# A two-layer decoder trunk on one core: c is copied whole from its PSUM bank, and the planner's price of a product gets 32 columns more

## The chip, the cores and the metric

The kernel runs on one core of a Trainium2 chip. A core has TensorE for matrix products (PE in the profile; PEld is its loading of stationary operands), VectorE (DVE), ScalarE (ACT), GpSimd (POOL) and SyncE (SP, which here only issues DMAs). They run from queues of their own, in order, and meet through semaphores. Matrix products write into PSUM, which has eight banks of 128 x 512 float32; everything else lies in SBUF. The metric is the device time of one execution in microseconds.

## The reference, cut to what matters

Two layers work on a sequence of 512 tokens with 1024 channels. Each normalizes x, multiplies by one wide matrix, feeds column groups to four mixers (latent attention, short convolution, spatial gate, block-sparse attention), gates each, and multiplies by W_out. The change sits at the beginning of the latent attention, where 416 columns (256 of cq, 128 of ckv, 32 of kr) become normalized inputs.

```python
h = rmsnorm(x, norm_g)
p = h @ w_in
(cq, ckv, kr, g_a, ...) = jnp.split(p, offs, axis=-1)
q = (rmsnorm(cq, mla_q_norm_g) @ mla_w_uq).reshape(B, S, MLA_HEADS, MLA_QK)
kv = (rmsnorm(ckv, mla_kv_norm_g) @ mla_w_ukv).reshape(...)
k_rope = rope(rmsnorm(kr, mla_k_rope_g)[:, :, None, :], positions)
...
return x + y @ w_out
```

## The kernel before, in words

Every float32 product is three passes: both factors are split into a rounded high part and a low part, and high x high, high x low and low x high are added in one bank (`mm3`, line 282). Names with h or whi are high parts, with l or wlo low parts. Weights come by DMA into raw buffers; ACT or DVE rounds the high part, DVE subtracts for the low part (`split_units`, line 442). Some combined weights of the second layer and of both output projections are added up in DRAM by DMAs ahead of their use (`t_sums`, line 356).

The order of all instructions on each engine is not written out. A planner in the kernel's Python makes it when the program is built: class `Order` (line 74) keeps a clock `now` for PE and one for each other engine, and chains of work are generators that wake when their inputs are planned to be ready. `Chain.pe` (line 198) puts a product into PE's queue once `now` has passed the chain's time by 80 ns, and moves `now` on by the product's price. That price is `cost(n)` for n columns (line 216); transposes of 128 columns have the fixed price 109 ns. `Chain.act` and `Chain.dve` price the other engines by columns. The main stream of big products has the lowest rank, so it fills in while the chains wait. Some tasks start at fixed moments of the planner's clock: `MIXT` (the spatial gate's mixing), `ROWT` (reciprocal roots for the rows of x), `COLT` (columns of parameters), line 36, and `TS0` (the weight sums), line 51. On the chip the queues only keep the order; the times follow from the hardware.

Buffers are handed out by class `Slots` (line 120): a chain that finds none waits in the plan until one is given back. The eight PSUM banks are three for accumulation (`accS`), two for transposes (`trS`) and three for the attention (`sS`). `t2S` is a pool of 11 SBUF tiles of 128 x 512 (line 248).

The stage around the change: the products with the 416 columns are called cq in the profile, a bank for each of the four groups of 128 tokens. In the first layer `c_first` (line 1704) makes all four at once, in three accS banks and one sS bank; in the second layer they follow one another in accS. For each group `low_chain` (line 983) copies the 384 columns of cq and ckv to ct, transposes ct in three products (cT), splits it into cTh and cTl, and multiplies it by the two up-projections (q, kv). Beside it `low_stats` (line 953) squares kr, ckv and cq with a running sum on ACT, copies kr to krt, forms the reciprocal roots on POOL (ms), and scales krt. The next main products, sq in the first layer and those named p in the second, need banks which the cq products hold.

Of the kernel before, what the change touches and what calls it, by code (L numbers as in the profile page):

```python
# [14 lines left out]
AF = mybir.ActivationFunctionType  # L15
# [5 lines left out]
NT = S // P  # L21
# [11 lines left out]
WSLACK = 0.0  # L33
AHEAD, URGENT, VSLACK = 4, 2, 300.0
NWARM, FILL, FILLEND = 6, 0.9, 15000.0
MIXT, MIXLAG, ROWT, COLT = 42000.0, 2000.0, 36000.0, 17500.0
KSPLIT, HMEAN = 6, 0.0
PAIRS = {}
LOPRIO = -5
# [8 lines left out]
SEQ1 = ['p11', 'ga0', 'p21', 'p3', 'ga1', 'p4', 'p2', 'ch0', 'p1', 'p22', 'cc0', 'gd0', 'gd1', 'su0', 'gc0', 'cb0', 'gb0', 'ch1', 'cc1', 'cb1', 'gb1', 'su1', 'gc1']  # L48
K0, K1, KK = (2, 3, 0, 1), (4, 5, 6, 7), (0, 2, 3, 1)
ZPROD = ("b11", "t3", "b21", "t4", "t2", "t1", "b22")  # L50
TS0 = 62000.0
TAIL = ((0, 256), (256, 512))

C_CQ, C_KV, C_GA, C_CH, C_CB, C_CC, C_GB = 0, 256, 416, 672, 928, 1184, 1440
# [111 lines left out]
class Chain:  # L166
# [6 lines left out]
    def _emit(self, e, cost, f, a, k):  # L173
        while max(self.t, self.o.clk[e] if self.lazy else 0.0) > self.o.now + self.slack:
            yield max(self.t, self.o.clk[e] if self.lazy else 0.0) - self.slack
        self.o.clk[e] = max(self.o.clk[e], self.t, self.o.now) + cost
        self.t = self.o.clk[e] + LAT
        f(*a, **k)  # L178
# [19 lines left out]
    def pe(self, cost, f, *a, **k):  # L198
        if self.t != self.pe_t:
            while self.t + PEMARGIN > self.o.now:  # L200
                yield self.t + PEMARGIN
        if self.o.now < self.o.fill_until:
            for _ in range(int((self.o.now - self.o.pe_end) * FILL / (430.0 if self.o.now < 9000.0 else 220.0))):
                self.o.fill()
        self.o.now += cost
        self.o.pe_end = self.o.now
        self.t = self.pe_t = self.o.now + PELAT
        f(*a, **k)  # L208
# [5 lines left out]


def cost(n):
    return max(n / 2.4, 107.0) + 2.0


@with_exitstack  # L220
def hybrid_trunk(ctx: ExitStack, tc: tile.TileContext, x, positions, norm_g, w_c, w_f, w_t, w_o, mla_q_norm_g,
# [3 lines left out]
    V, A, G, PE = nc.vector, nc.scalar, nc.gpsimd, nc.tensor  # L225
# [16 lines left out]
    o = Order()  # L242
# [5 lines left out]
    t2S = Slots(o, NT2, lambda name, dt=F32: t2p.tile([P, S], dt, tag="t2", name=name))  # L248
# [19 lines left out]
    def split2(ch, hi, lo, src):  # L268

        yield from ch.act(A.activation, hi, src, AF.Copy)  # L270
        yield from ch.dve(V.tensor_tensor, lo, src, hi.bitcast(F32), op=ALU.subtract)
# [10 lines left out]
    def mm3(ch, n, dst, sh, sl, mh, ml, first, last, go_on=False, low=None):  # L282

        c = cost(n)
        k = dict(skip_group_check=True) if go_on else {}
        yield from ch.pe(c, PE.matmul, dst, sh, mh, start=first, stop=False, **k)
        yield from ch.pe(c, PE.matmul, dst, sh, ml, start=False, stop=False, **k)
        if low is not None:
            yield from ch.wait(low)
        yield from ch.pe(c, PE.matmul, dst, sl, mh, start=False, stop=last, **k)  # L290
# [201 lines left out]
    def unit(ch, name, half=None):  # L492
        u = units[name]
        at[0] = max(at[0], u.idx)
        for v in order[u.idx:u.idx + AHEAD]:
            v.wanted = True
        yield from ch.wait(u.ready if half is None else u.half[half])
        return u.view()
# [4 lines left out]
    def shared(slots, n):  # L503

        left = [n]

        def put(ch):
            left[0] -= 1
            if left[0] == 0:
                slots.put(ch)  # L510
        return put
# [164 lines left out]
    for l in range(DEPTH):  # L676
        L = Layer()
# [38 lines left out]
    def pow_rstd(ch, dst, src, n):  # L716
        return ch.pow(G.tensor_tensor, dst, src, nhalf[:, :n], op=ALU.pow)
# [12 lines left out]
    def rv(i, t):  # L730
        return xv[:, i, t:t + 1]
# [170 lines left out]
    def rope(ch, x, nd, cb, sb, name):  # L902

        tab = yield from t2S.get(ch, f"rb{name}")
        x1, x2 = x[..., 0:nd], x[..., nd:2 * nd]
        shape = list(x1.shape)
        ta, tb = (tab[:, i * 256:i * 256 + free_size(x1)] for i in range(2))
        if len(shape) == 4:
            ta, tb = (z.rearrange("p (t h d) -> p t h d", t=NT, h=4) for z in (ta, tb))
            cb, sb = (z.unsqueeze(2).to_broadcast(shape) for z in (cb, sb))  # L910
        else:
            ta, tb = (z.rearrange("p (t d) -> p t d", t=NT) for z in (ta, tb))
        for out_, in0, in1, op in ((ta, x2, sb, ALU.mult), (tb, x1, sb, ALU.mult), (x1, x1, cb, ALU.mult),
                                   (x2, x2, cb, ALU.mult), (x1, x1, ta, ALU.subtract), (x2, x2, tb, ALU.add)):
            yield from ch.dve(V.tensor_tensor, out_, in0, in1, op=op)
        t2S.put(ch)
# [34 lines left out]


    def low_stats(L, t, a, t0, done):
        ch = Chain(o, t0)
        ssq, krt = L.ssq, L.krt
        ct = L.ct[t]
        for i, (c0, c1) in enumerate(((384, 416), (256, 384), (0, 256))):
            yield from ch.act(A.activation, junk[:, :c1 - c0], a[:, c0:c1], AF.Square, scale=(c1 - c0) ** -0.5,
                              accum_out=ssq[:, t, 2 - i:3 - i])
        yield from ch.act(A.activation, krt[:, t, :], a[:, 384:416], AF.Copy)  # L960
        done(ch)
        m = sm.tile([P, 8], F32, tag="ms", name=f"ms{t}_{L.l}")
        e1, e2 = EPS, EPS * EPS
        if L.l == 0:
            yield from ch.wait(v_ev)
            e1, e2 = rv(RE, t), rv(REE, t)
        yield from ch.dve(V.tensor_scalar, m[:, 0:2], ssq[:, t, 1:3], 1.0, e1, op0=ALU.mult, op1=ALU.add)
        yield from ch.dve(V.tensor_scalar, L.e2[:, t, :], ssq[:, t, 0:2], EPS, e2, op0=ALU.mult, op1=ALU.add)
        yield from pow_rstd(ch, m[:, 4:6], m[:, 0:2], 2)
        L.ms[t] = m  # L970
        o.set(L.stat[t], ch.t)
        yield from ch.dve(V.scalar_tensor_tensor, krt[:, t, :], in0=krt[:, t, :], scalar=m[:, 5:6], in1=L.gr,
                          op0=ALU.mult, op1=ALU.mult)
        L.kr_left -= 1
        if L.kr_left:
            return
        yield from ch.wait(rope_ev)
        yield from rope(ch, krt, 16, cosT, sinT, f"k{L.l}")
        yield from ch.wait(L.QK_ev)
        yield from ch.pool(G.tensor_copy, L.K[:, :, :, 64:96], krt.unsqueeze(2).to_broadcast([P, NT, 4, 32]))  # L980
        o.set(L.kr_ev, ch.t)

    def low_chain(L, t, a, t0, slots):
        ch = Chain(o, t0)
        l = L.l
        done = shared(slots, 2)
        ct = yield from t2S.get(ch, f"ct{t}_{l}")
        L.ct[t] = ct
        o.spawn(low_stats(L, t, a, t0, done))
        if o.clk["A"] < o.clk["V"]:  # L990
            yield from ch.act(A.activation, ct[:, :384], a[:, :384], AF.Copy)
        else:
            yield from ch.dve(V.tensor_copy, ct[:, :384], a[:, :384])
        done(ch)
        tp = yield from trS.get(ch, f"cT{t}_{l}")
        for k in range(3):
            yield from ch.pe(109.0, PE.transpose, tp[:, k * P:(k + 1) * P], ct[:, k * P:(k + 1) * P], ident)
        t2S.put(ch)
        c_h = yield from t2S.get(ch, f"cTh{t}_{l}", F32R)
        c_l = yield from t2S.get(ch, f"cTl{t}_{l}", F32R)  # L1000
        yield from split2(ch, c_h[:, :384], c_l[:, :384], tp[:, :384])
        trS.put(ch)
        q_ps = yield from sS.get(ch, f"q{t}_{l}")
        for k in range(2):
            uq_h, uq_l = yield from unit(ch, f"uq_{l}", k)
            yield from mm3(ch, 384, q_ps[:, :384], c_h[:, k * P:(k + 1) * P], c_l[:, k * P:(k + 1) * P],
                           uq_h[:, k, :], uq_l[:, k, :], k == 0, k == 1)
        o.spawn(q_chain(L, t, q_ps, ch.t))
        uk_h, uk_l = yield from unit(ch, f"ukv_{l}")
        kv_ps = yield from sS.get(ch, f"kv{t}_{l}")  # L1010
        yield from mm3(ch, 512, kv_ps, c_h[:, 256:384], c_l[:, 256:384], uk_h[:, 0, :], uk_l[:, 0, :], True, True)
        t2S.put(ch)
        t2S.put(ch)
        L.up_left -= 1
        if L.up_left == 0:
            units[f"uq_{l}"].slots.put(ch)
            units[f"ukv_{l}"].slots.put(ch)
        yield from kv_chain(L, t, kv_ps, ch.t)
# [668 lines left out]
    def main():  # L1687
        m = Chain(o)
# [207 lines left out]
        early_put(m)  # L1896
        for L in layers:
            l = L.l
            L.ct, L.ms, L.up_left = {}, {}, NT
            L.kr_ev, L.kr_left = Event(), NT  # L1900
            L.vn_alloc = Event()
            L.md_alloc = {"mq": Event(), "mk": Event()}
# [5 lines left out]
            for t in L.torder if l else ():  # L1908
                a = yield from accS.get(m, f"cq{t}_{l}")
# [10 lines left out]
            for n in SEQ1 if L.stok else SEQ:  # L1920
# [6 lines left out]
                elif n in TOKS:  # L1927
                    us = []
                    for ts in PAIRS.get((n, l), range(NT)):
                        ts = ts if isinstance(ts, tuple) else (ts,)  # L1930
                        a = {}
# [15 lines left out]
                else:  # L1947
                    a = yield from accS.get(m, f"{n}_{l}")
# [60 lines left out]
    def start():  # L2009
# [40 lines left out]
        o.spawn(main(), None, 10)  # L2050
    o.spawn(t_sums((0, z_src, "t", "b"), *((l, p_src, "p", "p") for l in STOK)), TS0, 4)
    o.spawn(start())
# [51 lines left out]
```

## Time and profile before

| | |
|---|---|
| median of 3 runs | 489.7 us (489.56 to 489.83) |
| profiled execution | 489.73 us, its span 488.0 us |
| PE, busy | 481.6 us, 99% of the span |
| DVE, busy | 400.9 us, 82% |
| ACT, busy | 329.9 us, 68% |
| POOL, busy | 104.4 us, 21% |
| DMA | 92.89 MB, mean 190 GB/s |
| PE clock granted | 0.999 of full speed |

The span is the time from the first to the last instruction of the program. A share is busy time over the span. In a row of the timeline the first number is the start in microseconds, the second the length, then engine, line, operation, and `out<-in` with the program's tile names; a bracket holds idle time before it and what ended it. The line is mostly that of a helper (L178 for ACT, DVE and POOL, L208 for PE), so tiles tell instructions apart. The chain that ended last is followed back from the last instruction to what released each step. A row of waits names who waited, for what, the total, the number of times and the longest. A row of a tile gives count, shortest, median and longest length in nanoseconds, first and last start, and the shapes. A row of windows gives the stretch, then busy time and count of PE, PEld, DVE, ACT and POOL, the granted clock, and DMA.

### The profile page before, as it was taken

What the parts mean: (1) busy time and instruction counts of PE and PEld (TensorE: products, weight loads), DVE (VectorE), ACT (ScalarE), POOL (GpSimd) and SP (SyncE); (2) the same over time, 40 slices, a digit from 0 to 9 for tenths busy, and PEclk for the clock granted to TensorE, in tenths of its full rate; (3) what the DMA queues carried; (4) which work ended last, traced back from release to release, by engine and by line L of the source; (5) the groups of instructions that cost most, each with busy time, mean ns of one, the idle gap of its engine ahead of it and who ended that gap; (6) DMA issues with size and microseconds to landing.
All of it is one profiled execution on the core that took longest, in us unless ns stands there. A gap on an engine that the chain in (4) does not pass through costs nothing.

```text
span 488.0 us, 7509 instructions
## 1 busy us (share of the span) xinstructions
PE 481.6 (99%) x2432; PEld 408.9 (84%) x2432; DVE 400.9 (82%) x893; ACT 329.9 (68%) x898; POOL 104.4 (21%) x172
## 2 busy tenths in 40 slices
PE   9999999999999999999999999999999999999997
PEld 7988888888887888888889988888888888888786
DVE  3698487668987899789998688979788998997993
ACT  5896837677546766457667788769675687666650
POOL 7855330710051210000031013620402200000000
PEclk9999999999999999999999999999999999999999
DMA  8742335897499888596574186786832744427762
GB/s 263 249 135 78 124 128 218 225 197 162 151 330 240 208 217 218 188 343 224 199 239 145 65 290 250 165 246 177 209 131 85 153 136 146 173 66 258 253 242 89
DMA packets 41904, 92.89 MB, mean 190 GB/s; under 512 B 7158, under 2 KB 23048, under 8 KB 41480
## 3 DMA queue, kind: packets, MB, share of 16 engines
q1 hardware_dynamic: 29168, 79.82, 47.3%
q0 software_dynamic: 12672, 12.58, 16.7%
q8 instruction: 19, 0.31, 0.2%
q14 instruction: 21, 0.17, 0.1%
q10 hardware_dynamic: 24, 0.01, 0.0%
HBM read 84.53 MB, written 33.03 MB: 241 GB/s over the span
## 4 chain that ended last, share of the span: by engine, by line
PE 91%; DVE 3%; ACT 2%; DMA 2%; SPq 1%; issue 1%; ACTq 0%
PE oy L208 6%; PE cq L208 6%; PE kv L208 6%; PE gb L208 5%; PE su L208 5%; PE cc L208 5%; PE sq L208 5%; PE gc L208 5%; PE ch L208 5%; PE ga L208 4%; PE oz L208 4%; PE cb L208 4%; PE py L208 3%; PE ox L208 3%; PE sa L208 3%; PE gd L208 3%
## 5 line engine op out<-in xcount | busy, mean ns | idle before, releaser
L178 ACT ACTIVATE pa<-pa,mna 128x128 f32<-128x128 f32 (+3 forms) x53 | 27.8, 554 | 5.6 <-DVE mna L178 5.5
L178 ACT ACTIVATE pd<-pd,mnd 128x384 f32<-128x384 f32 (+3 forms) x49 | 25.8, 548 | 3.2 <-DVE mnd L178 2.9
L178 ACT ACTIVATE pha<-pTa 128x512 fp32r<-128x512 f32 (+3 forms) x32 | 13.9, 434 | 20.6 <-PE pTa L208 20.4
L178 ACT ACTIVATE phd<-pTd 128x512 fp32r<-128x512 f32 (+3 forms) x32 | 13.8, 434 | 16.1 <-PE pTd L208 15.9
L178 DVE CUSTOM_DVE_ANT_0 pa<-sa,maskb,rs_q 128x512 f32<-128x512 f32 (+3 forms) x32 | 16.6, 544 | 6.2 <-PE sa L208 3.2
L178 DVE TENSOR_TENSOR wlo_p<-raw_p,whi_p 128x512 fp32r<-128x512 f32 x28 | 19.1, 698 | 2.7 <-ACT whi_p L178 2.6
L178 ACT ACTIVATE whi_t<-raw_t 128x512 fp32r<-128x512 f32 x31 | 18.2, 619 | 4.5 <-DMA raw_t<-t 4.5
L208 PE MATMUL cq<-whi_c,hTh 128*128 128x416 f32 x64 | 20.8, 370 | 0.0
L178 DVE TENSOR_TENSOR wlo_t<-raw_t,whi_t 128x512 fp32r<-128x512 f32 x32 | 20.7, 679 | 0.0
L208 PE MATMUL cq<-wlo_c,hTh 128*128 128x416 f32 x64 | 20.0, 359 | 0.0
L178 DVE TENSOR_TENSOR pla<-pTa,pha 128x512 fp32r<-128x512 f32 (+3 forms) x32 | 15.4, 485 | 5.6 <-ACT pha L178 5.6
L208 PE MATMUL cq<-whi_c,hTl 128*128 128x416 f32 x64 | 19.8, 355 | 0.0
L178 POOL TENSOR_TENSOR rs_mk<-rs_mk,nhalf 128x16 f32<-128x16 f32 x2 | 6.5, 3243 | 56.3 <-DVE rs_mk L178 56.3
L178 DVE CUSTOM_DVE_ANT_0 pd<-sd,maskb,rs_mq 128x512 f32<-128x512 f32 (+3 forms) x32 | 17.0, 545 | 1.6 <-PE pTd L208 1.0
L178 DVE TENSOR_TENSOR pld<-pTd,phd 128x512 fp32r<-128x512 f32 (+3 forms) x32 | 15.1, 485 | 3.1 <-ACT phd L178 3.0
L178 POOL TENSOR_SCALAR xss<-xss 128x1 f32<-128x1 f32 x4 | 2.7, 668 | 69.6 <-ACT jk L178 65.3
L372 POOL DMA_DIRECT2D t<-in_w_o_dram x16 | 17.0, 1341 | 2.4 <-DMA t<-t 2.3
L178 DVE TENSOR_TENSOR wlo_b<-raw_b,whi_b 128x512 fp32r<-128x512 f32 x24 | 16.0, 682 | 0.1
L178 ACT ACTIVATE whi_b<-raw_b 128x512 fp32r<-128x512 f32 x23 | 13.9, 622 | 3.1 <-DMA raw_b<-in_w_o_dram 3.0
L178 ACT ACTIVATE whi_p<-raw_p 128x512 fp32r<-128x512 f32 x22 | 13.2, 625 | 3.9 <-DMA raw_p<-in_w_t_dram 3.9
L208 PE MATMUL pTd<-ident,pd 128*128 128x128 f32 x80 | 14.1, 272 | 0.6 <-ACT pd L178 0.6
L208 PE MATMUL pTa<-ident,pa 128*128 128x128 f32 x80 | 14.0, 273 | 0.0
(473 smaller groups left out, 1846.8 us busy)
## 6 DMA issues: line engine op xcount, KB each, us to landing
t<-in_w_o_dram POOLq DMA_DIRECT2D x16, 512.0 KB, 8.3
raw_t<-t SPq DMA_DIRECT2D x16, 512.0 KB, 4.0
raw_b<-in_w_o_dram SPq DMA_DIRECT2D x12, 512.0 KB, 4.0
t<-in_w_o_dram SPq DMA_DIRECT2D x8, 512.0 KB, 4.9
p<-in_w_t_dram POOLq DMA_DIRECT2D x8, 512.0 KB, 14.0
t<-t SPq DMA_DIRECT2D x8, 512.0 KB, 4.7
raw_p<-p SPq DMA_DIRECT2D x8, 512.0 KB, 3.2
ys<-ysc SPq DMA_DIRECT2D x14, 256.0 KB, 5.0
```

The lines of the kernel that those rows point to most:

```text
L178: f(*a, **k)
L208: f(*a, **k)
L372: nc.gpsimd.dma_start(src(l, n, j), src(l, y, j), accum_op=ALU.add, max_dma_last_dim=1024)
```

## The change

`low_chain` copies all 416 columns into ct and gives the bank back right after that copy. `low_stats` is started after the copy instead of before it, and reads ct. The copy of kr to krt on ACT goes: the scaling of krt on DVE reads ct. ct itself is given back after both the transposes and that scaling. Apart from this, `cost(n)` is priced as 32 columns more without the constant 2 ns, and four fixed moments of the planner's clock are set later.

```diff
-MIXT, MIXLAG, ROWT, COLT = 42000.0, 2000.0, 36000.0, 17500.0
+MIXT, MIXLAG, ROWT, COLT = 44000.0, 2000.0, 37700.0, 18000.0
...
-TS0 = 62000.0
+TS0 = 65000.0
...
 def cost(n):
-    return max(n / 2.4, 107.0) + 2.0
+    return max((n + 32) / 2.4, 108.0)
...
     def low_stats(L, t, a, t0, done):
         ch = Chain(o, t0)
         ssq, krt = L.ssq, L.krt
-        ct = L.ct[t]
         for i, (c0, c1) in enumerate(((384, 416), (256, 384), (0, 256))):
             yield from ch.act(A.activation, junk[:, :c1 - c0], a[:, c0:c1], AF.Square, ...)
-        yield from ch.act(A.activation, krt[:, t, :], a[:, 384:416], AF.Copy)
-        done(ch)
...
-        yield from ch.dve(V.scalar_tensor_tensor, krt[:, t, :], in0=krt[:, t, :], scalar=m[:, 5:6], in1=L.gr,
+        yield from ch.dve(V.scalar_tensor_tensor, krt[:, t, :], in0=a[:, 384:416], scalar=m[:, 5:6], in1=L.gr,
                           op0=ALU.mult, op1=ALU.mult)
+        done(ch)
...
     def low_chain(L, t, a, t0, slots):
-        done = shared(slots, 2)
+        done = shared(t2S, 2)
         ct = yield from t2S.get(ch, f"ct{t}_{l}")
-        L.ct[t] = ct
-        o.spawn(low_stats(L, t, a, t0, done))
         if o.clk["A"] < o.clk["V"]:
-            yield from ch.act(A.activation, ct[:, :384], a[:, :384], AF.Copy)
+            yield from ch.act(A.activation, ct[:, :416], a[:, :416], AF.Copy)
         else:
-            yield from ch.dve(V.tensor_copy, ct[:, :384], a[:, :384])
-        done(ch)
+            yield from ch.dve(V.tensor_copy, ct[:, :416], a[:, :416])
+        slots.put(ch)
+        o.spawn(low_stats(L, t, ct, ch.t, done))
...
-        t2S.put(ch)
+        done(ch)
```

More of the change, by code (lines that the diff above doesn't have):

```diff
@@ L1898, in main @@
             l = L.l
-            L.ct, L.ms, L.up_left = {}, {}, NT
+            L.ms, L.up_left = {}, NT
             L.kr_ev, L.kr_left = Event(), NT
```

## The prediction

> **What bounds the kernel now.** I read the page's busy times first, then what TensorE (PE) waited for, then the chain that ended last, and only then the instructions of the one stage where the change acts.
>
> ```profile
> PE 481.6 (99%) x2432; PEld 408.9 (84%) x2432; DVE 400.9 (82%) x893; ACT 329.9 (68%) x898; POOL 104.4 (21%) x172
> PE 91%; DVE 3%; ACT 2%; DMA 2%; SPq 1%; issue 1%; ACTq 0%
> ```
>
> PE is busy for 481.6 of 488.0 us and carries 91% of the chain that ended last. The change neither adds nor removes a needed product, so only time in which PE stands still can be won. The next rows are the waits of PE, all of them, and the last stretch.
>
> ```profile
> PE warm L2019 <- DVE ones L2017: 1.1, 1, 1.1
> PE pTd L208 <- ACT pd L178: 0.6, 1, 0.6
> PE sq L208 <- ACT krt L178: 0.6, 1, 0.6
> PE gd L208 <- DVE zz L178: 0.3, 1, 0.3
> PE oz L208 <- DVE wlo_b L178: 0.3, 1, 0.3
> ...
> 475.80:488.00 12.20, 8.79 (x51) 7.57 (x49) 3.86 (x7) 0.00 (x0) 0.00 (x0) 0.96 0.25 90
> ```
>
> The first wait is the start-up and the last stretch (8.79 of 12.20 us busy) is the run-out of results; the change touches neither. The other four waits together are 1.8 us. A shown matmul also covers its drain, so part of a stall hides inside "busy"; I therefore look at starts in the chain of waits. One of the four belongs to the edited code: sq, the first product after the first stage, waits for krt, the copy in low_stats that gives a bank of c back.
>
> ```profile
> 28.82 0.76 ACT cTh L178 x2
> ...
> 31.04 0.38 ACT ct L178
> 31.42 0.18 ACT junk L178 x2
> 31.60 0.10 ACT krt L178
> 31.69 0.04 issue
> 31.74 0.97 PE sq L208 x3
> 32.70 1.05 PE q L208 x6
> 33.75 0.33 PE cT L208 x3
> 34.08 0.70 PE sq L208 x3
> 34.78 0.69 PE kv L208 x3
> ```
>
> The chain leaves PE here, for ACT's queue, and comes back through krt. The instructions of PE, DVE and ACT around it:
>
> ```profile
> 26.27 0.55 DVE L178 COPY ct<-cq 128x384 f32<-128x384 f32 x1
> 27.37 0.68 DVE L178 TENSOR_TENSOR yTl<-raw_sq,yTh 128x512 fp32r<-128x512 f32 x1
> 30.64 0.68 DVE L178 TENSOR_TENSOR yTl<-raw_sq,yTh 128x512 fp32r<-128x512 f32 x1
> 31.24 0.54 DVE L178 TENSOR_TENSOR cTl<-cT,cTh 128x384 fp32r<-128x384 f32 x1
> ...
> 31.48 0.21 ACT L178 ACTIVATE krt<-cq 128x32 f32<-128x32 f32 x1
> 31.55 0.65 ACT L178 ACTIVATE whi_sq<-raw_sq 128x512 fp32r<-128x512 f32 x1
> ...
> 29.26 0.43 PE L208 MATMUL q<-whi_uq,cTh 128*128 128x384 f32 x1
> 30.65 0.49 PE L208 MATMUL cT<-ident,ct 128*128 128x128 f32 x3
> 31.74 0.50 PE L208 MATMUL sq<-yTh,hTh 128*128 128x512 f32 x1 [0.60 <-ACT krt L178]
> 34.62 0.40 PE L208 MATMUL kv<-whi_ukv,cTh 128*128 128x512 f32 x1
> ```
>
> **The change, part by part.** I make the sum against this execution: 489.73 us, of which 488.0 are the span; it lies 0.03 us from the median, 489.7.
>
> *The bank comes back after the copy.* Before, a bank is held by ct, three squares and the krt copy; its last reader ended at 31.48 + 0.21 = 31.69. After, the copy alone holds it: 26.27 + 0.55 = 26.82, and some 0.03 us more for 32 of 384 columns. From 29.26 (first q) to 34.62 (first kv) is 5.36 us. The work in it, by the chain's clean pieces, is two q groups (2 x 1.05), two cT groups (2 x 0.33) and two sq groups (2 x 0.70): 4.16 us. So 1.20 us are lost, partly before sq, partly as q waits for its operands from 29.26 on. With the bank free, the first sq group can stand in front of or between the q products: its weights' low half was ready at 27.37 + 0.68 = 28.05, the second group's at 31.32 and q's second operand at 31.78, which is when a PE without the stall would ask for them. The squares now start behind the copy; on ACT's queue that costs nothing, since in the chain above (31.04, 31.42) a square follows its copy already, and behind them only the ms products on POOL wait, which no product in this stretch reads. I take the full 1.20; the bounds are 0 (PE next waits for those DVE outputs) and 1.20.
>
> *ACT and DVE.* Eight krt copies go (0.10 us each on the chain, 0.8 in all), 32 columns more are copied eight times, and 24 squares now read SBUF.
>
> ```profile
> L178 ACT ACTIVATE junk<-cq x24: 192/281/420, 26.9 to 280.1; 128x32 f32<-128x32 f32 x8, 128x128 f32<-128x128 f32 x8, 128x256 f32<-128x256 f32 x8
> L178 ACT ACTIVATE junk<-x x16: 401/404/419, 7.1 to 24.5; 128x256 f32<-128x256 f32 x16
> 24.40:36.60 12.20, 11.60 (x61) 9.84 (x60) 11.76 (x29) 11.64 (x47) 6.61 (x15) 1.00 0.49 135
> ```
>
> A 256-wide square from SBUF took 404 ns and the longest from PSUM 420, so I price the move at nothing, with bounds of -0.8 and +0.5 us of ACT time; neither is on PE's path once the bank no longer hangs on it. It matters only in the one stretch where ACT (11.64) and DVE (11.76 of 12.20) are nearly full. [...]
>
> *ct is held longer*, until the krt product instead of until its transposes.
>
> ```profile
> L178 DVE SCALAR_TENSOR_TENSOR krt<-krt,ms,gr_b x8: 238/243/244, 37.2 to 282.7; 128x32 f32<-128x32 f32 x8
> ...
> 34.84 0.54 DVE L178 TENSOR_TENSOR cTl<-cT,cTh 128x384 fp32r<-128x384 f32 x1
> 35.08 0.39 PE L208 MATMUL kv<-whi_ukv,cTl 128*128 128x512 f32 x1
> 41.17 0.33 PE L208 MATMUL q<-whi_uq,cTh 128*128 128x384 f32 x1
> ```
>
> The first krt product ran at 37.2, so all four ct are still held when the fourth cTl is due at 34.84; with eight cTh and cTl that makes 12 buffers where 11 exist. The fourth cTl then waits for the first kv (35.08 + 0.39 = 35.47) and is 0.6 us late. Its reader came at 41.17, 5.8 us after; sq products cover it. Cost 0, bounds 0 to 0.6. Nothing is queued behind it that PE needs sooner.
>
> *The product's estimate.* It only moves the planner's order. By line 217, 512 columns go from 215.3 to 226.7 ns, 416 from 175.3 to 186.7, 384 from 162 to 173.3, 256 from 109 to 120, 128 from 109 to 108; transposes keep a literal 109.
>
> ```profile
> 211.04 5.44 PE oz L208 x24
> 253.28 2.27 PE cq L208 x12
> ```
>
> Measured: 5.44 / 24 = 226.7 and 2.27 / 12 = 189 ns. The new estimate is right; the old one let PE run 5.3% slower than planned, so every chain had 53 ns per us more than the planner meant to give it. That reserve goes. DVE is not underestimated: a 512-wide subtraction is planned at 68 + 1.047 x 512 = 604 ns, and above the cTl starts 31.24 - 30.64 = 0.60 us after the 512-wide yTl before it. So I take 0 for the reordering. Its bounds: the other three waits gone, 0.6 + 0.3 + 0.3 = 1.2 us won; 4.6 us lost (rival below). [...]
>
> *The due times* (MIXT, ROWT, COLT, TS0) grow by 2.9 to 4.8% with the planner's clock, so their work keeps its place among the products: 0. DMA issues of the weight sums begin at the same product, but their fixed gaps now span 5% fewer products; they drift forward by 5% of the time since TS0, some 4 us after 80 us. I put no price on it; it is the part that I can least follow.
>
> Sum: 489.73 - 1.20 + 0 + 0 = 488.5 us.
>
> **The rivals.**
>
> *Slower: the reserve was needed.* For it: products that wait for long chains stand where the planner thinks them just ready.
>
> ```profile
> 151.79 0.33 PE L208 MATMUL sd<-mk1d,mq1d 128*128 128x384 f32 x1
> 157.17 0.27 PE L208 MATMUL pTd<-ident,pd 128*128 128x128 f32 x1
> ```
>
> From scores to the transposes of a head (pa, pd to pTa, pTd) go about 5.4 us (151.79 to 157.17); 5.3% of that is 0.29 us, in 16 heads 4.6 us. Against it: of 16 heads one waited at all (0.6 us). If three quarters of the 4.6 are paid, the time is 489.73 - 1.20 + 3.45 = 492.0 us. It ends on the other side of before once more than 1.2 us, about a quarter, is paid, and beyond 0.2% from 2.2 us on, about a half.
>
> *No difference: DVE takes the gain back.* For it: DVE has 11.76 of 12.20 us in this stretch, and a PE that is 1.2 us earlier asks for yTl and cTl the earlier. Against it: the second yTl was done at 31.32 and the second sq group ran at 34.08, 2.8 us later. Time: 489.73 - 0.2 = 489.5 us.
>
> *The change doesn't do what it says:* the planner may put sq where it was, since other chains (q, cT) have priority over it. Then only the wait moves and the time is also near 489.5; I count it with the one before.
>
> **How the numbers follow.** The forecast has a chance of 0.45 (its own range 487.0 to 488.7), the slower rival 0.38, the two without difference 0.17. About 0.2% (1 us) is what can be told from no change. From these cases: faster 0.45, same 0.17, slower 0.38. The low end takes the forecast and the 1.2 us of other waits, 487.3, and 0.3 for stalls that hide in "busy": 487.0. The high end lies where nearly nine tenths of the reserve is paid: 492.6.
>
> **What would show it.** Right: PE's list of waits has no sq behind krt or ct; first q to first kv take near 4.2 us; copies of 416 columns, no krt from cq; PE's total of waits near 2.3 us. Reserve lost: new PE waits on pa, pd, pla, pld, cTl or wlo tiles, spread over both layers, of 0.1 to 0.5 us each. DVE takes it back: PE waits on yTl or cTl between 29 and 37 us. The prediction is wrong if the first stage gains and the loss lies in one place far from it, above all at a weight's DMA that collides with the shifted weight sums.

## The result and the profile after

The changed kernel takes 501.85 us (median of six executions, 498.98 to 506.77) against 489.67 us (489.56 to 490.02): a ratio of 1.0229, 95% interval 1.0205 to 1.0254. The ratio is taken from the fast runs and leaves out the execution of 506.77 us, more than 1.5% above the fastest, which the median of six still counts. The profiled execution is the fastest of them, 498.98 us with a span of 497.3 us. The forecast was 488.5 us, and the time lies far above the high end of the range.

First the busy times and the shares of the chain that ended last, of after; then its waits of PE:

```profile
PE 485.1 (98%) x2432; PEld 408.0 (82%) x2432; DVE 401.6 (81%) x891; ACT 330.4 (66%) x892; POOL 103.0 (21%) x172
PE 72%; DMA 11%; DVE 10%; ACT 5%; issue 1%; POOL 1%; SPq 0%; DVEq 0%; ACTq 0%
```

```profile
PE pTd L208 <- ACT pd L178: 1.5, 1, 1.5
PE tmkd L208 <- DVE mk L178: 1.5, 2, 0.7
...
PE sa L208 <- DVE lo1a L178: 0.8, 1, 0.8
PE oy L208 <- DVE xr L178: 0.7, 1, 0.7
...
```

No engine got more instructions. PE carries 72% of the chain instead of 91%, and DMA 11% instead of 2%. The wait of sq for krt is gone, as forecast; in its place stand eleven kinds of waits (besides the start-up's warm) all over the run, on DVE and ACT, none of them for a tile of the edited code.

A busy PE hides part of a stall: in both traces a product of 512 columns is shown 389 ns long, while the next one starts 227 ns after it (medians). The reader of a bank follows the shown end: in before the last product of an oz bank starts at 213.37 us and is shown for 0.39 us, and ACT reads the bank from 213.79 us on. So I also use PE's starts: the time from the first matmul's start to the last one's, minus what the 2,432 products need at (n + 32) / 2.4 ns for n columns (110 ns for 128 columns). The medians from start to start, the same in both traces, are 227 ns for 512 columns, 190 for 416, 175 for 384, 119 for 256 and 108 for 128. That need is about 471.7 us for every kernel here. What is left, the excess, is time that PE lost: 11.4 us before and 20.6 us after. The difference, 9.2 us, is the difference of the two profiled executions (9.25 us). Counted in stretches of 12.2 us, the stage of the change wins 0.9 us (1.56 to 0.67, between 24.4 and 36.6 us), and these lose most against before: 134 to 146 us 1.0, 183 to 195 us 1.9, 317 to 342 us 2.6, 354 to 366 us 0.9, 390 to 403 us 0.9, and the run-out from 464 us on 2.1.

**How one place loses.** The largest of these, 317 to 342 us, is 2.6 of the 9.2 us. First the medians from issue to landing, of before and then of after:

```profile
t<-in_w_o_dram POOLq DMA_DIRECT2D x16, 512.0 KB, 8.3
raw_t<-t SPq DMA_DIRECT2D x16, 512.0 KB, 4.0
...
raw_p<-p SPq DMA_DIRECT2D x8, 512.0 KB, 3.2
```

```profile
t<-in_w_o_dram POOLq DMA_DIRECT2D x16, 512.0 KB, 10.2
raw_t<-t SPq DMA_DIRECT2D x16, 512.0 KB, 5.5
...
raw_p<-p SPq DMA_DIRECT2D x8, 512.0 KB, 7.1
```

The row with POOLq is the adding DMAs of the weight sums, which POOL issues; raw_p and raw_t are loads of combined weights, on SP's queue. In before, two raw_p were issued from 308.12 us on, ahead of a group of three adding DMAs. These are the issues on SP's and on POOL's queue in before:

```profile
308.12 0.79 SPq L295 DMA_DIRECT2D raw_p<-p  x2
...
309.21 3.24 POOL L372 DMA_DIRECT2D t<-in_w_o_dram  x3
```

In after the order is turned, and a group of four goes first. POOL's row, the step of the chain, and then DVE and PE in after:

```profile
307.55 4.27 POOL L372 DMA_DIRECT2D t<-in_w_o_dram  x4
```

```profile
311.42 7.11 DMA raw_p<-p
```

```profile
314.27 1.29 DVE L178 TENSOR_TENSOR wlo_ch<-raw_ch,whi_ch 128x512 fp32r<-128x512 f32 x2
318.62 0.43 DVE L178 CAST whi_p<-raw_p 128x512 fp32r<-128x512 f32 x1 [3.07 <-DMA raw_p<-p]
...
326.59 0.71 DVE L178 SCALAR_TENSOR_TENSOR lo1a<-t1a,pcol,hi1a 96x512 fp32r<-96x512 f32 x1
...
325.33 0.39 PE L208 MATMUL ch<-hTh,wlo_ch 128*128 128x512 f32 x1
326.05 0.50 PE L208 MATMUL sa<-hi1a,hi0a 96*128 96x512 f32 x1 [0.33 <-ACT hi1a L178]
327.36 0.50 PE L208 MATMUL sa<-lo1a,hi0a 96*128 96x512 f32 x1 [0.81 <-DVE lo1a L178]
```

raw_p takes 7.11 us to land, and DVE's queue stands 3.07 us behind it. From 318.62 us on DVE works without a gap, but lo1a, the low half that the score products sa need, comes late all the same, and PE waits 0.81 us for it. Two other places, as the chain shows them:

```profile
176.45 8.70 DMA ysc<-yad
...
388.29 0.66 issue
388.95 3.43 POOL rs_mk L178
```

At 176 us a store of 256 KB (yad) lands only after 8.70 us, DVE waits 2.83 us for it, and pTd stalls PE for 1.50 us, until 188.7. At 388 us the root rs_mk (3.43 us) starts on POOL only after another root (rs_mq, 3.85 us) and the issue of an adding DMA (0.7 us), and tmkd stalls PE until 394, at the end for 0.75 us.

### The profile page after: what moved, and what is told of

Same layout as the page of the kernel before. It is cut to its first block, busy times and chain, and to the rows that moved or that the text cites. A ratio compares the mean times of both kernels' runs of the same rounds, so it can differ in the third digit from the quotient of the medians.

```text
span 497.3 us, 7486 instructions
## 1 busy us (share of the span) xinstructions
PE 485.1 (98%) x2432; PEld 408.0 (82%) x2432; DVE 401.6 (81%) x891; ACT 330.4 (66%) x892; POOL 103.0 (21%) x172
## 4 chain that ended last, share of the span: by engine, by line
PE 72%; DMA 11%; DVE 10%; ACT 5%; issue 1%; POOL 1%; SPq 0%; DVEq 0%; ACTq 0%
PE cq L208 7%; PE kv L208 5%; PE oy L208 5%; PE gb L208 4%; PE ga L208 4%; PE sq L208 4%; PE cb L208 4%; PE su L208 3%; PE gc L208 3%; DMA ysc<-yad 3%; PE ch L208 3%; PE pz L208 2%; PE sa L208 2%; PE ox L208 2%; PE oz L208 2%; PE cc L208 2%
## 5 line engine op out<-in xcount | busy, mean ns | idle before, releaser
L178 ACT ACTIVATE pa<-pa,mna 128x256 f32<-128x256 f32 (+3 forms) x54 | 28.2, 551 | 4.6 <-DVE mna L178 4.5
L178 ACT ACTIVATE phd<-pTd 128x512 fp32r<-128x512 f32 (+3 forms) x32 | 13.7, 433 | 11.4 <-PE pTd L208 11.0
L178 POOL TENSOR_TENSOR rs_mq<-rs_mq,nhalf 128x16 f32<-128x16 f32 x2 | 6.7, 3372 | 51.7 <-ACT pa L178 33.1
L178 ACT ACTIVATE whi_p<-raw_p 128x512 fp32r<-128x512 f32 x24 | 14.5, 622 | 2.3 <-DMA raw_p<-p 2.3
L208 PEld LDWEIGHTS pTd<-ident,pd 128*128 128x128 f32 x80 | 10.2, 140 | 5.9 <-ACT pd L178 2.2
```

## The experiments

Ratios are against runs of the kernel before on the same chip. The expectations name theories by letters. At the start there were three: A, the reserve that the old price left is lost (in its narrow form, reserve for late DMAs); B, the edit of `low_chain` does it, by holding ct or by the order that it makes alone; C, the weight sums run denser against PE's work. Later came D, late DMAs at the head of in-order queues cost the time; L, the order is a lottery; and Q, the order of ACT's and DVE's queues is bad in itself, DMAs aside. Kernels without the adding DMAs, or with 8 of their 128 rows, leave out that part of the combined weights, and only their time is used.

### The two parts alone

bank_only takes the edits of `low_chain` and `low_stats` with the old price and due times; cost_only takes the price and the due times with the old functions. bank_only against after:

```diff
-MIXT, MIXLAG, ROWT, COLT = 44000.0, 2000.0, 37700.0, 18000.0
+MIXT, MIXLAG, ROWT, COLT = 42000.0, 2000.0, 36000.0, 17500.0
...
-TS0 = 65000.0
+TS0 = 62000.0
...
-    return max((n + 32) / 2.4, 108.0)
+    return max(n / 2.4, 107.0) + 2.0
```

> The edits of low_chain and low_stats alone, on the kernel before; the old price of a product and the old due times. Theory A (the loss comes from the new price, which takes the 5.3% that every chain had in hand): 488 to 490 us, the wait of sq behind krt gone. Theory B (the loss comes from ct being held longer, or from the order that this edit alone makes): 495 us or more, with the waits of the changed kernel.

> The new price and the new due times alone; low_chain and low_stats as before. Theory A (lost reserve): 498 to 504 us, TensorE waits spread over both layers and a chain that holds some 10% DMA. Theory B (the edit of low_chain): 488 to 491 us.

Measured: bank_only 493.02 us, 1.0072 (1.0045 to 1.0099); cost_only 491.32 us, 1.0026 (1.0012 to 1.0039). Both lose, and 0.7% and 0.3% don't make 2.3%. Neither time lies in a range that A or B gave for it. If the bank's part had its 1.2 us and nothing else, bank_only would be faster than before. PE's two longest waits in it:

```profile
PE sd L208 <- DVE mnd L178: 2.2, 1, 2.2
PE py L208 <- ACT hi0a L178: 1.8, 1, 1.8
```

They begin at 156 and 332 us, before other products than those that wait in after. So the edit moves the order even with the old price, and neither A nor B can be the whole: the price alone costs 1.3 us, the edit alone 3.5 us.

### The shift of the due times and of the sums

after_due is after with the four due times of before (the first two edits above). after_gaps stretches the fixed gaps between the sums' DMAs by 5.3%:

```diff
-        gap = 4000.0 if len(streams) == 1 else 3000.0
+        gap = 4212.0 if len(streams) == 1 else 3159.0
...
-                o.set(tsum_ev[l, n, j], o.now + 10000.0)
+                o.set(tsum_ev[l, n, j], o.now + 10530.0)
...
-            yield o.now + (8000.0 if len(streams) == 1 else 0.0)
+            yield o.now + (8424.0 if len(streams) == 1 else 0.0)
```

> The changed kernel with the four old due times (42000, 36000, 17500 and 62000 ns). If the due times are part of the cause: 490 to 494 us. If they aren't (Theory D): 496 to 502 us, the same kinds of waits.

> The changed kernel, the fixed gaps of the weight sums (4000, 3000, 8000 and 10000 ns of the planner's clock) 5.3% longer, so that as many products as before lie between two of them. Theory C (the denser weight sums collide with the weights' DMAs): 490 to 494 us, the share of DMA in the chain back near 2%. Theory A (lost reserve): 498 us or more, since only these DMAs move.

Measured: after_due 500.68 us, 1.0232 (1.0188 to 1.0276); after_gaps 500.06 us, 1.0206 (1.0183 to 1.023). Neither brings the time back. The due times cost nothing that can be told, and the sums' pace is not the cause: C falls.

### Telling the planner of later transfers

after_dma and before_dma let the planner expect a landing after 4 us instead of 2; after_w does so for weight loads alone; after_dma2 is after_dma with the 2 us kept between 215 and 262 us of the planner's clock:

```diff
-        ch.t = o.clk["D"] + 2000.0
+        ch.t = o.clk["D"] + (4000.0 if o.now > 15000.0 else 2000.0)
```

after_charge lets the planner count the sums' traffic on its one DMA clock, for the copy and for the adding DMA:

```diff
-                o.clk["D"] = max(o.clk["D"], o.now) + 1500.0
+                o.clk["D"] = max(o.clk["D"], o.now) + 3000.0
...
                 o.clk["G"] = max(o.clk["G"], o.now) + 1000.0
+                o.clk["D"] = max(o.clk["D"], o.now) + 3000.0
```

> The changed kernel, but the planner expects each DMA that a chain waits for to land 4000 instead of 2000 ns after its transfer (from 15 us on). Theory A in its narrow form (what is missing is reserve for DMAs that land late, and in-order queues behind them): 489 to 494 us, DMA in the chain below 5%. If the reserve is missing for the short chains through ACT and DVE instead: 498 us or more, with TensorE still waiting on pd, lo1a, mk and x.

> The kernel before, with the planner expecting DMAs 2000 ns later, as in after_dma. Theory D (late DMAs at the head of in-order queues cost time in every order of this planner, and the order before was lucky): no gain or a small one, 488 to 491 us, its share of DMA in the chain at most 2%. Theory L (any new order of the changed kernel is better than its own, the lateness is not what matters): 491 to 496 us, since the order before is broken up as well.

> The changed kernel, with the later landing assumed for the weights' loads alone, and not for x, the norm's gains, the y halves or the mixing weights. Theory D: near after_dma, 490 to 494 us; if also the stall at the layers' border goes, 488 to 490 us. If the y halves (ysc) carry the loss: 496 us or more.

> after_dma, but with the later landing not assumed between 215 and 262 us of the planner's clock, the border of the two layers, where after_dma stalled for some 5 us. Theory D: 487 to 490 us, better than the kernel before by up to 2 us. Theory L (lottery): 490 to 496 us.

> The kernel after, with the planner charging 3000 ns of its one DMA clock for each copy and for each adding DMA of the weight sums, in place of 1500 ns for the copy and nothing for the adding one. If the loss comes from transfers that the planner takes for free: 489 to 493 us, and less DMA in the chain of waits than the 11% of after. If any such edit merely draws another order: anything from 491 to 500 us, and the share of DMA in the chain does not go with the time.

Measured: after_dma 492.42 us, 1.0054 (1.0035 to 1.0073); before_dma 494.16 us, 1.01 (1.0071 to 1.0128); after_w 494.78 us, 1.0098 (1.0063 to 1.0132); after_dma2 490.12 us, 1.0016 (0.9993 to 1.0039); after_charge 500.0 us, 1.0195 (1.0177 to 1.0213). A later landing takes most of the loss out of after, but costs before 1%: it is no repair as such. In after_dma the stalls in the middle are gone, and one at the layers' border is new:

```profile
PE hT L208 <- ACT a L178: 2.4, 1, 2.4
```

after_dma2, which leaves that border alone, comes to within the measurement of before. Charging the planner for the sums' traffic does not bring the time back, although DMA's share of the chain falls from 11% to 5%; the second of its two expectations came true. So late transfers matter, as D says, but D is no rule: before_dma, which D put at 488 to 491 us, takes 494.16 us, in the range of L, and after_w lies just above D's 490 to 494 us. The planner's landing time is not what decides.

### Taking the traffic away

before_noacc and after_noacc leave out the 24 adding DMAs (the first line here); after_tiny puts the second line in its place, 8 of 128 rows on the same queue with the same waits:

```diff
-                nc.gpsimd.dma_start(src(l, n, j), src(l, y, j), accum_op=ALU.add, max_dma_last_dim=1024)
+                nc.gpsimd.dma_start(src(l, n, j)[0:8, :], src(l, y, j)[0:8, :], accum_op=ALU.add, max_dma_last_dim=1024)
```

> The kernel before without the 24 adding DMAs of the weight sums on POOL's queue (they are left out, so products that use a sum get one summand alone; the output isn't the reference's); every other instruction and the planner's clock as before. It gives the base for after_noacc. Theory D (in the order before hardly anything is late): 486 to 490 us, its own stalls of 1 to 3 us are all that can go.

> The changed kernel without the same 24 adding DMAs, output as for before_noacc. Theory D (the adding DMAs make weights and y halves land late, and in-order queues carry that to TensorE): 487 to 492 us, within 3 us of before_noacc. Theory Q (the order of ACT's and DVE's queues is bad in itself, DMAs aside): 497 us or more, still 8 to 12 us above before_noacc.

> The kernel after, in which each adding DMA of the weight sums carries 8 of its 128 rows: every issue, every wait on POOL's queue and the order of all engines stay, but nearly all of the adding traffic goes (so the combined weights are left wrong in the other rows; time only). If the traffic slows the transfers that PE's path needs: 490 to 494 us, as without the adding DMAs (492.2), and raw_p lands in under 5 us. If it is POOL's queue, whose later instructions stand behind the issues and behind waits for copies: 497 us or more, and raw_p may land early all the same.

Measured: before_noacc 489.45 us, 0.9991 (0.9977 to 1.0004); after_noacc 492.21 us, 1.0049 (1.0031 to 1.0067); after_tiny 493.36 us, 1.0057 (1.0037 to 1.0078). In before these DMAs cost nothing that can be told; in after they cost some 9 us. after_tiny keeps every issue and wait of after and its order; its raw_p lands in 3.2 us, and its DVE row stands without a wait:

```profile
raw_p<-p SPq DMA_DIRECT2D x8, 512.0 KB, 3.2
```

```profile
312.11 0.41 DVE L178 CAST whi_p<-raw_p 128x512 fp32r<-128x512 f32 x1
```

POOL waits for the copies t no less than in after. In these rows, of after and then of after_tiny, the first number behind the bar is POOL's time in the issues, the second the mean of one in ns, and then comes the wait:

```profile
L372 POOL DMA_DIRECT2D t<-in_w_o_dram x16 | 17.0, 1378 | 47.1 <-DMA t<-t 47.1
L372 POOL DMA_DIRECT2D t<-in_w_o_dram x16 | 13.3, 1045 | 51.3 <-DMA t<-t 51.3
```

So it is the traffic in the main, and not POOL's queue. The queue is not held wholly fixed, though: an issue takes a quarter less time with 8 rows.

The excess shows where the traffic matters: 20.6 us in after, 13.4 us in after_tiny. Between 183 and 195 us it falls from 2.1 to 0.1 us, between 317 and 342 us from 2.7 to 1.0 us, between 354 and 366 us from 0.9 to 0.2 us. Between 134 and 146 us it stays (1.1 us), and in the run-out 1.7 of 2.1 us stay. So not every place that loses hangs on the traffic.

Between 295 and 330 us the queue of the adding DMAs (q0) and that of the other transfers (q1) took these shares of the 16 DMA engines, first in after, then in after_tiny:

```profile
q1 hardware_dynamic: 1525, 6.05, 48.2%
q0 software_dynamic: 2112, 2.10, 38.8%
```

```profile
q1 hardware_dynamic: 1358, 5.10, 42.2%
q0 software_dynamic: 192, 0.13, 3.2%
```

2.10 MB of adding took 38.8%, 6.05 MB of the rest 48.2%: per byte 2.3 times as much. Together the two queues took 87.0% of the 16 engines in after and 45.4% in after_tiny, and raw_p landed after 7.1 and 3.2 us. How the engines divide their time between the queues is not shown.

### Another order and nothing else

`PEMARGIN` is the 80 ns by which the planner lets a product trail its inputs. With 60 or 100 ns PE has the same 2,432 products; what changes is the order and, since the planner also chooses between ACT and DVE by its clocks, which of the two does some small steps (after has 891 instructions on DVE and 892 on ACT, after_m60 886 and 891). The kernels named m60 and m100 have it so, after_m60 for one:

```diff
-LAT, PELAT, SLACK, PEMARGIN = 130.0, 220.0, 300.0, 80.0
+LAT, PELAT, SLACK, PEMARGIN = 130.0, 220.0, 300.0, 60.0
```

after_krt has the copy of kr on ACT again, out of ct, and gives ct back right after it, not after the product of krt on DVE:

```diff
+        yield from ch.act(A.activation, krt[:, t, :], a[:, 384:416], AF.Copy)
+        done(ch)
```

> The changed kernel with TensorE's margin in the planner 100 instead of 80 ns: a new order, but no better knowledge of DMAs. Theory L (the order is a lottery): anywhere from 490 to 500 us. Theory D: 496 to 502 us, with 6% or more DMA in the chain.

> The changed kernel, with the copy of kr to krt back (from ct, on ACT), so that ct is given back without waiting for the root. If holding ct is the cause: 490 to 494 us. If not: 495 to 502 us.

> The kernel after, with the lead of 80 ns that a product gives its inputs cut to 60: an edit that draws another order and nothing else. If the order of after is an unlucky one among many: 491 to 496 us, as with 100 ns (493.2). If the new price by itself costs time: 497 us or more.

> The kernel before, with the lead of 80 ns raised to 100. If the order of before is a lucky one: 491 to 496 us, like the other drawn orders. If the old price with its reserve makes good orders in general: 489 to 490.5 us.

> The bank edit alone (old price, old due times), with the lead of 60 ns. If the bank edit's 1.2 us is real and the order decides the rest: 488.5 to 489.5 us where no stall above 1 us is left in PE's row of starts, and 1.2 us more for each further place where PE waits. If only price and edit together make the gain with 60 ns: 491 us or more.

> The price and the due times alone, with the lead of 60 ns; the bank is held by the krt copy as in before. If the bank edit is what after with 60 ns gained (489.0 against 490.1 us): 489.7 to 490.5 us, and PE's starts lose again some 1.5 us between 24 and 37 us. If the order alone decides: anything from 489 to 494 us.

The column of the excess is that of the profiled execution; the last one counts PE's products between the transposes t1a and the first scores sa near 326 us, besides 18 py that stand there in all of them.

| kernel | median us | ratio (95%) | excess of PE's starts, us | raw_p lands, us | products before sa |
|---|---|---|---|---|---|
| after | 501.85 | 1.0229 (1.0205 to 1.0254) | 20.6 | 7.1 | 18 ch |
| after_krt | 497.61 | 1.0162 (1.0138 to 1.0186) | 19.4 | 8.3 | 18 ch |
| after_m100 | 493.18 | 1.0069 (1.0045 to 1.0093) | 14.9 | 7.6 | 24 ch, 27 py |
| after_m60 | 488.95 | 0.9981 (0.9971 to 0.9991) | 10.3 | 6.9 | 24 ch, 27 py |
| before_m100 | 489.68 | 0.9994 (0.998 to 1.0008) | 11.4 | 3.2 | 24 ch, 30 py |
| bank_m60 | 491.42 | 1.004 (1.0021 to 1.0058) | 14.7 | 3.2 | 24 ch, 27 py |
| cost_m60 | 489.62 | 1.0001 (0.9988 to 1.0014) | 10.6 | 3.2 | 24 ch, 27 py |

With 60 ns, a smaller reserve still, the same change is 0.2% faster than before: this is the version that beats both kernels. So neither the edit nor the new price costs 12 us by itself; the order does that they draw together with 80 ns. And cost_m60 against after_m60 tells what the bank edit is worth where little else is in the way. The waits of PE in after_m60, all of them, and the one that cost_m60 has besides the same wait of warm:

```profile
PE warm L2017 <- DVE ones L2015: 1.1, 1, 1.1
PE cq L208 <- ACT hTh L178: 0.3, 1, 0.3
PE py L208 <- DVE x L178: 0.2, 1, 0.2
PE oy L208 <- DVE wlo_t L178: 0.2, 1, 0.2
```

```profile
PE sq L208 <- ACT krt L178: 0.7, 1, 0.7
```

Without the bank edit sq waits for krt again, and PE's excess between 24.4 and 36.6 us is 1.77 us; with it 0.70 us. Over the whole run the two differ by only 0.3 us (10.6 and 10.3), so in the profiled executions most of that gain goes again in other places.

The last column of the table shows what differs at 326 us. Between the transposes t1a and the first scores sa, PE's queue holds 18 py and 18 ch in after, but 18 py, 24 ch and 27 py in after_m60: sa stands 33 products, some 7.5 us, later there. Yet after_m60 has nearly the same late raw_p (6.9 us) and the same kind of wait on DVE:

```profile
313.91 0.76 DVE L178 CAST whi_p<-raw_p 128x512 fp32r<-128x512 f32 x2 [2.85 <-DMA raw_p<-p]
```

The largest loss of PE near it is 0.4 us. So three cases stand beside each other: late transfer and early reader (after) stall PE at sa; late transfer and late reader (after_m60) do not; early transfer and early reader (after_tiny) do not either. All kernels with the 18-ch order and the full traffic (after, after_due, after_gaps, after_charge, after_krt) take 497.6 us or more; of the others none takes over 494.8 us. The mark is no law: after_dma2 has sa after 12 ch already and a raw_p of 7.4 us, and takes 490.12 us.

In bank_m60 the place is another again, from 221 us on in the output projection:

```profile
PE oz L208 <- DVE wlo_b L178: 2.1, 2, 1.5
```

Its 491.42 us also lie in the range of the other expectation (491 us or more, if price and edit make the gain only together), so bank_m60 alone doesn't decide between the two. And before_m100, at 489.68 us, is in the range for "the old price makes good orders in general", not in that for a lucky order of before. That can't be the whole: with the old price before_dma takes 494.16 us and bank_only 493.02 us, and with the new one after_m60 takes 488.95 us and cost_m60 489.62 us. As a tendency it is not excluded: the kernels with the old price and the full traffic lie between 489.7 and 494.2 us, those with the new one between 489.0 and 501.9 us.

## Why the prediction was wrong

*The bank comes back after the copy: right in the gain, wrong in the way.* The stage's window, then the squares and the copies, and then the first product each of kv and of sq in after:

```profile
24.40:36.60 12.20, 12.04 (x66) 10.85 (x65) 11.29 (x29) 11.66 (x42) 6.33 (x13) 1.00 0.52 139
```

```profile
L178 ACT ACTIVATE junk<-ct x24: 213/308/420, 27.9 to 284.7; 128x32 f32<-128x32 f32 x8, 128x128 f32<-128x128 f32 x8, 128x256 f32<-128x256 f32 x8
...
L178 DVE COPY ct<-cq x7: 576/580/592, 27.0 to 281.1; 128x416 f32<-128x416 f32 x7
...
30.92 0.39 PE L208 MATMUL kv<-whi_ukv,cTh 128*128 128x512 f32 x1
...
33.34 0.48 PE L208 MATMUL sq<-yTh,hTh 128*128 128x512 f32 x1
```

PE is busy for 12.04 of 12.20 us where it was 11.60. I took 1.20 us; the starts show 0.9 us in after and 1.07 between cost_m60 and after_m60 (1.77 to 0.70), and the ratios of these two, each against before on its own chip, differ by 0.2%, some 1 us. But I expected sq to move in front of or between the q products, and it did not. The first sq started at 31.74 us before, behind one group of six q products and one of cT; in after it starts at 33.34 us, behind two such q groups, one kv group and two cT groups. The gain comes because q and kv work fills the time in which PE stood. after_m60, bank_only and bank_m60 have the same order there, and before, cost_only and cost_m60 the old one, so it goes with the bank edit. That the planner would not put sq forward was in the rival of no difference; that the stage gains all the same was not, and there the forecast had luck. The view that I named, first q to first kv, can't be used, since kv now comes before sq. In the result the gain is drowned.

*ACT and DVE: right as a term.* The 256-wide squares stay at 420 ns at most; the median, that of the 128-wide ones, rises from 281 to 308 ns, 27 ns where I had priced the move at nothing. By this my estimate is some 0.4 us of ACT in all (27 ns on 16 narrow squares), within the bound of 0.5 us, and ACT's busy time stays (329.9 to 330.4 us).

*ct is held longer: no sign of a cost.* No product waits for cTl, and giving ct back early (after_krt) leaves 1.6% of loss.

*The due times: no sign of a cost*, by after_due. The drift of the sums, on which I put no price, is not the cause by after_gaps.

*The product's estimate: here it failed.* The sentence "So I take 0 for the reordering", with bounds of -1.2 and +4.6 us, was the wrong step. The price itself is right (226.7 ns planned for 512 columns, 227 ns from start to start in both traces), and the reserve that the old one left was not needed, as cost_m60 and after_m60 show, which lose nothing without it. But I priced the reordering as a stretching of the same order, every chain 5% nearer to its reader. It is another order: readers and transfers move against each other by several us, as sa by 33 products. All kernels here with the full traffic span 488.95 to 501.85 us, so bounds that held would have been about -1 and +12 us; only these runs, made afterwards, show that size. The bank edit draws a new order too, which I had counted in its own stage only: bank_only loses 0.7% with the old price.

*The slower rival* fails as a mechanism, although the sign was its. It wanted small waits spread over the attention heads. Some of its signs are there: in after PE waits on pd, pa, pld and wlo_t tiles, 2.6 us in all, and in cost_only 0.9 us on pd. But the largest of them, 1.5 us on pd, is the one behind the late store of yad; cost_only, nearly its pure case, loses 1.3 us; and the lead of 60 ns, with less reserve still, loses nothing. The sentence on what would make the prediction wrong was half right: transfers collide with the adding DMAs, but in several places, and not because the sums are shifted.

*What stays open.* Why the planner puts sa ahead of the last ch at 80 ns and not at 60 or 100 wasn't followed through its choices. The 3 us that after_tiny still loses lie in waits that after has too (tmkd, oy, py), without the traffic; that their order alone causes them is argued, not shown. How often the planner draws an order as poor as this can't be told from so few: the changed kernel was drawn with three leads, and before with two (60 ns was not tried there). So it is open, too, whether the old price, with its reserve, draws good orders more often.

## What to carry to other kernels

Where a program orders the instructions, an edit of a price or of a buffer's life is two changes: its own effect, and a new order. Price the second by drawing it: change a neutral constant by a little, with and without the edit, and take the spread before believing a per cent. And look for late transfers that an order happens to tolerate: before's adding DMAs cost nothing that can be told (0.9991 without them) until another order put readers behind them.

## What the runs showed of the hardware

In after_gaps a lower clock followed a stall of PE, so that more was lost there than the stall's length. PE stood still for 1.9 of the 3 us between 324 and 327 us. In its windows of 1 us the first busy time is PE's, and the third number from the end is the granted clock:

```profile
324.00:325.00 1.00, 0.48 (x3) 0.06 (x1) 1.00 (x3) 0.99 (x3) 0.00 (x0) 1.00 0.93 344
325.00:326.00 1.00, 0.43 (x1) 0.19 (x1) 1.00 (x2) 1.00 (x3) 0.00 (x0) 1.00 0.71 275
326.00:327.00 1.00, 0.20 (x2) 0.13 (x2) 1.00 (x4) 0.97 (x7) 0.62 (x2) 1.00 0.00 0
327.00:328.00 1.00, 1.00 (x6) 0.90 (x7) 0.68 (x3) 0.55 (x4) 0.99 (x2) 1.00 0.08 16
328.00:329.00 1.00, 1.00 (x6) 0.90 (x5) 1.00 (x5) 0.55 (x1) 0.77 (x3) 0.59 0.21 26
329.00:330.00 1.00, 1.00 (x4) 0.81 (x3) 0.36 (x2) 1.00 (x5) 0.71 (x2) 0.50 1.12 168
330.00:331.00 1.00, 1.00 (x3) 0.72 (x3) 0.00 (x0) 0.36 (x2) 0.00 (x0) 0.50 1.12 176
331.00:332.00 1.00, 1.00 (x6) 0.94 (x5) 0.23 (x1) 0.00 (x0) 0.00 (x0) 0.70 0.86 127
```

Against the full clock the rows from 328 to 332 us lack 0.41 + 0.50 + 0.50 + 0.30 = 1.71 us, on top of the stall. A lower clock does not follow every stall: in after_due PE stood still for 2.5 us between 94 and 98 us, and the clock stayed at 1.00 then and behind it:

```profile
94.00:96.00 2.00, 0.68 (x4) 0.38 (x3) 0.00 (x0) 0.24 (x1) 0.00 (x0) 1.00 1.23 466
96.00:98.00 2.00, 0.80 (x5) 0.67 (x6) 0.82 (x3) 2.00 (x9) 0.00 (x0) 1.00 0.81 242
98.00:100.00 2.00, 2.00 (x14) 1.74 (x13) 1.60 (x4) 1.95 (x7) 1.01 (x1) 1.00 1.14 246
```

What decides whether the clock falls is not shown.

The clock also goes with uneven times. Six of the ten executions of after_dma2 have a mean clock of 0.999 or 1.000 and take 488.66 to 490.70 us; the four with 0.996 or 0.997 take 492.14 to 492.90 us. The lost clock, 0.3 to 0.4% of 490 us, is some 1.5 to 2 us of the 3 us between the two groups; where the rest comes from is not shown. In after the profiled execution has a mean clock of 1.000 and takes 498.98 us, one with 0.992 takes 502.96 us; but one with 0.997 takes 502.50 us, so there the clock is not all. In the runs of before the mean clock was 0.998 to 1.000.
